# A two-layer mixer with an expert-lookup feed-forward: gate products ordered behind the low parts, wider one-hots, modulation steps spread

## The chip, the core and the metric

The kernel is one program on one core of a Trainium2 chip. The core has five engines that run side by side, each taking its own instructions in order: TensorE (PE, matmuls; PEld is its weight load), VectorE (DVE), ScalarE (ACT), GpSimd (POOL) and SyncE (SP), which here issues most transfers between DRAM and on-chip memory. The metric is the device time of one execution in microseconds (us), taken as the median of runs. A profiler's trace of one execution is beside it.

## The reference

Two layers work on 256 tokens `x` of width 1024 and, in the first layer, on 256 context tokens as well. Each layer is a mixer of four branches, then a feed-forward that looks up experts; both are scaled and shifted by six modulation vectors per stream.

```python
for l in range(DEPTH):                      # 2
    mx = (jax.nn.silu(c) @ mod_w[l] + mod_b[l])[:, None, :]      # six vectors of 1024
    mc = (jax.nn.silu(c_ctx) @ mod_w[l] + mod_b[l])[None, None, :]
    ...
    yx, yc = hybrid_mixer(hx, hc, ...)
    x = x + g1x * yx
    hx2 = rmsnorm(x, norm2_w[l]) * (1.0 + sc2x) + sh2x
    x = x + g2x * peer_ffn(hx2, peer_w_q[l], peer_keys[l], peer_u[l], peer_v[l])

def one_block(xt):                          # of peer_ffn, 128 tokens
    q = (xt @ w_q).reshape(128, 8, 2, 64)
    s = jnp.einsum('thpd,hpkd->thpk', q, keys)
    s1, i1 = lax.top_k(s[:, :, 0], 16)
    s2, i2 = lax.top_k(s[:, :, 1], 16)
    ...                                     # the 16 best of 16 x 16 sums, per head
    g = jax.nn.softmax(top_s, axis=-1)
    act = gelu(einsum('td,thkd->thk', xt, u[eidx]))
    return einsum('thk,thkd->td', g * act, v[eidx])
```

There are 128 x 128 experts, and each token has 8 heads of 16 chosen ones.

## The kernel before

**Dense experts.** The kernel doesn't gather the rows of `u` and `v` for most token tiles. It computes all 16384 experts in 128 blocks of 128 and multiplies by a gate matrix that is zero for experts not chosen. The first pass (`block` in `peer_u`, the U pass) computes `gelu(u x)` for block e and writes it to DRAM (`act_d`). The second pass (`peer_v`, the V pass) loads it back as tile `a`, multiplies it by the gates `G` (line 1241, the gate product), splits the product into `wh` and `wl`, and multiplies by block e of `v` into `pacc`, which stays in PSUM. In layer 0 three token tiles go this way (`n` = 384) and one goes through gathered rows (`sparse`, lines 900 to 931): 256 gathers of 512 KB, a multiply on VectorE for each, spread over the blocks of both passes. In layer 1 there are two tiles (`n` = 256).

**Two halves of each weight.** A weight block of 128 x 1024 floats is loaded into `raw` (three buffers) by `next_w`, and `split_w` (lines 150 to 158) makes `hi` on ScalarE and the low part `lo = raw - hi` on VectorE (line 157), five buffers each. Each product takes three matmuls: both high, and the two mixed ones. A V block is 18 matmuls of 512 columns in layer 0 and 12 in layer 1. The handle `lo_turn["last"]` keeps the last low part that was traced.

**Blocks and pairs.** In layer 0 a tile `a` holds two blocks (a pair), in layer 1 four (a quad, two gate products). There are four buffers for `a` in layer 0 and two in layer 1, where every fourth quad stays on chip instead (`keep`). The load of a later `a` (line 1213, on SP's queue) is traced behind the `wl` (line 1246) that is the last reader of its buffer. `G` comes in four parts for every 16 blocks.

**Who orders the work.** The text of the kernel gives the order of tracing. The framework's scheduler then sets the order on each engine by its own estimate of when an instruction is ready, so one that is ready early may be put in front. `with tc.issue_after(ins):` adds an edge of order to what is traced inside it: on the engine of `ins`, it is issued behind `ins`, with no wait for its end. The kernel uses it already for the multiplies of the gathered rows (lines 919 and 929).

**Gates.** For each token tile `route` finds the chosen experts; then `hot` (16 times a tile, in the U pass) builds, for 8 tokens, the one-hot of the second index (`a2`) and that of the first index (`a1`), and from the latter its products with the high and the low part of the weight (`bh`, `bl`). `eight` multiplies them on TensorE into the gates of those tokens, which go to `g_d`. The indices and weights lie along the free axis in `ix`, which `look2` fills from PSUM.

**Modulation.** Four of layer 0's segments and two of layer 1's are computed in layer 0's mixer without TensorE's weight path: `mod_seg` (lines 242 to 277) loads a half segment in eight pieces of 256 KB and folds each into `macc` on VectorE for both streams; `finish` sums over partitions by four transposes for each stream on TensorE. The generator stops twice in a segment. `with_mods` takes one step of it at the given indices of a filler generator (`MODS_AT`, and line 709); what is left is taken behind the last merge (line 846), ahead of the output projection `out_proj`. Of the 13 steps that exhaust the six segments, layer 0's mixer takes 2 + 3 + 4 + 2 = 11 at indices and the others behind the last merge.

Of the kernel before, what the change touches and what calls it, by code (L numbers as in the profile page):

```python
# [19 lines left out]
P = 128  # L20
# [10 lines left out]
SP = 1  # L31
NG = 4
AB = (4, 2)
MODS_AT = (((1, 5, 8), (1, 6, 12, 17), (0, 2)), ((1, 8), (1, 12), (2,)))
GS = 16384.0
MLA_SCALE = 96.0 ** -0.5

# [76 lines left out]
def hybrid_peer(ctx, tc, resin, cvec, modw, modb, nw, win, uq, uk, uv, colw, nab, retl, gnw,  # L114
# [159 lines left out]
    def with_mods(gen, at, mod):  # L274
        for i, x in enumerate(gen):
            if i in at:
                next(mod, None)
            yield
# [98 lines left out]
    def mixer(l, hT, st, s_acc, pre):  # L377
# [328 lines left out]
                yield  # L706
            yield from proj_tok(B_NV, range(4), lambda t2, p: act.activation(nv[:, t2:t2 + 2, :], p, AF.Copy))

        weave(retention(), with_mods(fill_na(), (0, 3, 6) if not full else (0, 5), mods), 0.7)
        rs.close()  # L710

        acp = s_acc.enter_context(tc.tile_pool(name=f"acp{l}", bufs=1, reuse_waits="tile", side="right"))
# [220 lines left out]
    def peer_u(l, hT, rp, ap_, pre, kp_, normed, xrow, vps):  # L933
# [30 lines left out]
        def route(tt):  # L964
# [95 lines left out]
            def look2():  # L1060
                if tt not in dense:
                    wn = T[tt, "wn"]
                    spw["idx"] = kp_.tile([P, P], U32, name="idx")
                    spw["wgt"] = kp_.tile([P, P], F32, name="wgt")
                    dve.scalar_tensor_tensor(wn[:, 0], wn[:, 0], float(P), wn[:, 1], op0=OP.mult, op1=OP.add)
                    dve.tensor_copy(spw["idx"], wn[:, 0])
                    dve.tensor_copy(spw["wgt"], wn[:, 2])
                    return
                tp = ps_o("idxT")
                for q in range(3):  # L1070
                    pe.transpose(tp[:, q * P:(q + 1) * P], T[tt, "wn"][:, q], ident)
                ix = up2.tile([P, 4, P], F16, tag="ixT", bufs=2, name="ixT")
                act.activation(ix[:, 0:2].rearrange("p q t -> p (q t)"), tp[:, :256], AF.Copy)
                act.activation(ix[:, 2], tp[:, 256:384], AF.Copy, scale=GS)
                dve.scalar_tensor_tensor(ix[:, 3], tp[:, 256:384], GS, ix[:, 2], op0=OP.mult, op1=OP.subtract)
                T[tt, "ix"] = ix
            add(400, look2)
            if tt not in dense:
# [1 line left out]
            for c in range(8):  # L1080
                def gsub(c=c):
                    T[tt, "stage"] = up2.tile([P, P, 16], F32, tag="gst", bufs=2, name="gst")
                add(0, gsub)
                for j in range(2):
                    def hot(c=c, j=j):
                        t0 = c * 16 + j * 8
                        ix = T[tt, "ix"]
                        cur = [ix[:, q, t0:t0 + 8].rearrange("p (g t) -> p g t", t=2)[:, :, None, :]
                               .to_broadcast([P, 4, P, 2]) for q in range(4)]
                        irep = irep2[:, None].to_broadcast([P, 4, P, 2])  # L1090
                        a2, a1, bh, bl = (up2.tile([P, 4, P, 2], F16, tag=nm, bufs=nb, name=nm)
                                          for nm, nb in (("a2", 2), ("a1", 1), ("bh", 2), ("bl", 2)))
                        dve.tensor_tensor(a2, irep, cur[1], op=OP.is_equal)
                        dve.tensor_tensor(a1, irep, cur[0], op=OP.is_equal)
                        dve.tensor_tensor(bh, a1, cur[2], op=OP.mult)
                        dve.tensor_tensor(bl, a1, cur[3], op=OP.mult)
                        T[tt, "hot", c, j] = a2, bh, bl, T[tt, "stage"]

                    def eight(c=c, j=j):
                        a2, bh, bl, stage = T.pop((tt, "hot", c, j))  # L1100
                        for q in range(2):
                            gp = ps_s("gps")
                            for i in range(4):
                                t = q * 4 + i
                                o = gp[:, i * P:(i + 1) * P]
                                at = a2[:, t // 2, :, t % 2]
                                pe.matmul(o, at, bh[:, t // 2, :, t % 2], start=True, stop=False)
                                pe.matmul(o, at, bl[:, t // 2, :, t % 2], start=False, stop=True)
                            tc0 = j * 8 + q * 4
                            act.activation(stage[:, :, tc0:tc0 + 4],  # L1110
                                           gp.rearrange("p (t i) -> p i t", t=4), AF.Copy)
                        if j == 1:
                            sync.dma_start(g_d[tt * 8 + c], stage)

                    add(2800, hot)
                    if "late" in T:
                        add(0, T.pop("late"))
                    T["late"] = eight
# [70 lines left out]
    def peer_v(l, vp, tail, s_up, keep, sparse_step, gen):  # L1189
# [42 lines left out]
        for e in range(P):  # L1232
# [3 lines left out]
            if e % na == 0:  # L1236
                ia = e // na
                a, G = keep[ia] if ia in keep else loads.pop(ia), loads["G", i]
                for j in range(0, na, 2):
                    a4 = a[:, j:j + 2].rearrange("p j (c t) -> p j c t", t=16)  # L1240
                    dve.tensor_tensor(a4, a4, G[:, :, e % ng + j:e % ng + j + 2].rearrange("p c j t -> p j c t"),  # L1241
                                      op=OP.mult)
                wh = vp.tile([P, na, n], F32R, tag="wh", bufs=3, name="wh")
                wl = vp.tile([P, na, n], F32R, tag="wl", bufs=3, name="wl")
                act.activation(wh, a, AF.Copy)
# [256 lines left out]
```

## Time and profile before

| | |
|---|---|
| median of 3 runs | 3072.34 us (3067.71 to 3074.73) |
| profiled execution, its own time | 3068.09 us |
| its span, first to last instruction | 3066.3 us |
| TensorE matmuls open | 2912.8 us, 95% of the span |
| TensorE weight loads | 84% |
| VectorE busy | 2287.7 us, 75% |
| ScalarE busy | 1293.5 us, 42% |
| GpSimd busy | 442.8 us, 14% |
| transfers | 718.42 MB, mean 234 GB/s |
| chain that ended last | PE 34%, transfers 16% (`a<-act_d` alone 10%), DVE 15% |

How to read it: matmuls are pipelined and overlap, so a busy TensorE need not be one at its best. The chain is followed back from the last instruction, at each step to what released it. The share of a transfer in it is time in which nothing else stood between the kernel and its end.

### The profile page before, as it was taken

Reading aid. Unit: us, or ns where it says so; the run is one execution under the profiler, and the core shown is the slowest. Engines: PE = TensorE matmul, PEld = TensorE weight load, DVE = VectorE, ACT = ScalarE, POOL = GpSimd, SP = SyncE. Lnnn points to the kernel's source line nnn. Section 1 sums busy time; section 2 is a strip of 40 time slices with the busy share of each in tenths; the row PEclk is TensorE's granted clock in tenths of the full one; section 3 lists DMA queues with packets and bytes.
Section 4 is the critical chain, followed back from the end, with each engine's and each line's share of the span. In section 5 each row is a group of like instructions: output and inputs, shape, how many; then the busy total and the mean of one; then the engine's idle time right before and its main releaser. Section 6 shows DMA issues by size and latency. Waiting matters only on the chain.

```text
span 3066.3 us, 46551 instructions
## 1 busy us (share of the span) xinstructions
PE 2912.8 (95%) x17771; PEld 2563.2 (84%) x17771; DVE 2287.7 (75%) x4013; ACT 1293.5 (42%) x1910; POOL 442.8 (14%) x378
## 2 busy tenths in 40 slices
PE   8999999799999999998888999999999999999998
PEld 6877767798889989986677777988899999988887
DVE  6768793658989999666666777777659798576665
ACT  6344442433343434332232233545554545554443
POOL 0200011001222232232222322101100000000000
PEclk9999999899999999999999999999999999999999
DMA  6343333435797979998888887465455867898874
GB/s 250 108 145 124 117 124 103 149 116 201 238 331 245 351 258 351 359 380 300 295 303 300 316 275 264 163 211 174 138 167 188 272 213 269 288 312 290 272 257 152
DMA packets 242080, 718.42 MB, mean 234 GB/s; under 512 B 24384, under 2 KB 68544, under 8 KB 236736
## 3 DMA queue, kind: packets, MB, share of 16 engines
q1 hardware_dynamic: 204704, 580.69, 56.1%
q0 software_dynamic: 36864, 134.23, 12.3%
q8 instruction: 139, 2.28, 0.3%
q14 instruction: 85, 0.70, 0.1%
q10 hardware_dynamic: 288, 0.52, 0.0%
HBM read 633.56 MB, written 81.79 MB: 233 GB/s over the span
## 4 chain that ended last, share of the span: by engine, by line
PE 34%; DMA 16%; DVE 15%; issue 4%; ACT 2%; POOL 0%; DVEq 0%; SPq 0%; POOLq 0%; ACTq 0%
PE va L1229 12%; DMA a<-act_d 10%; DVE lo L157 4%; PE H L358 4%; PE H L360 4%; PE H L359 4%; DMA raw<-in_ub_dram 4%; DVE spacc L930 2%; DVE wl L1246 2%; DMA mraw<-in_modw_dram 1%; PE proj L358 1%; PE proj L359 1%; PE proj L360 1%; DVE gat L920 1%; ACT hi L154 1%
## 5 line engine op out<-in xcount | busy, mean ns | idle before, releaser
L154 ACT ACTIVATE hi<-raw 128x1024 fp32r<-128x1024 f32 x676 | 715.7, 1060 | 1345.6 <-DMA raw<-in_vb_dram 451.6
L157 DVE TENSOR_TENSOR lo<-raw,hi 128x1024 fp32r<-128x1024 f32 x680 | 832.2, 1226 | 375.2 <-ACT hi L154 370.9
L358 PE MATMUL H<-h2h,hi 128*128 128x384 f32 (+1 forms) x2048 | 647.9, 316 | 14.7 <-ACT ast L1146 14.7
L360 PE MATMUL H<-h2h,lo 128*128 128x384 f32 (+1 forms) x2048 | 637.1, 312 | 2.5 <-DVE lo L157 2.4
L359 PE MATMUL H<-h2l,hi 128*128 128x384 f32 (+1 forms) x2048 | 637.7, 311 | 0.0
L1229 PE MATMUL va<-lo,wh 128*128 128x512 f32 x1280 | 408.3, 398 | 55.5 <-DVE lo L157 55.1
L358 PEld LDWEIGHTS H<-h2h,hi 128*128 128x128 f32 x2048 | 388.3, 190 | 20.2 <-ACT ast L1146 18.2
L1229 PE MATMUL va<-hi,wh 128*128 128x512 f32 x1280 | 403.4, 394 | 1.6 <-ACT keep L1146 1.5
L1229 PE MATMUL va<-hi,wl 128*128 128x512 f32 x1280 | 402.8, 394 | 0.0
L360 PEld LDWEIGHTS H<-h2h,lo 128*128 128x128 f32 x2048 | 387.6, 189 | 4.1 <-DVE lo L157 3.6
L359 PEld LDWEIGHTS H<-h2l,hi 128*128 128x128 f32 x2048 | 388.6, 190 | 0.0
L1229 PEld LDWEIGHTS va<-lo,wh 128*128 128x128 f32 x1280 | 241.8, 191 | 119.0 <-DVE lo L157 70.3
L1229 PEld LDWEIGHTS va<-hi,wh 128*128 128x128 f32 x1280 | 243.1, 190 | 53.9 <-ACT keep L1146 2.4
L358 PE MATMUL proj<-hh,hi 128*128 128x256 f32 (+1 forms) x808 | 283.1, 351 | 5.3 <-ACT hh L349 3.4
L1229 PEld LDWEIGHTS va<-hi,wl 128*128 128x128 f32 x1280 | 244.0, 191 | 52.0
L359 PE MATMUL proj<-hl,hi 128*128 128x256 f32 (+1 forms) x808 | 276.4, 342 | 0.0
L360 PE MATMUL proj<-hh,lo 128*128 128x256 f32 (+1 forms) x808 | 275.8, 342 | 0.0
L1241 DVE TENSOR_TENSOR a<-a,G 128x768 f32<-128x768 f32 (+1 forms) x112 | 92.2, 842 | 208.6 <-DMA a<-act_d 200.1
L910 POOL DMA_INDIRECT gat<-in_urow_dram,idx x128 | 161.1, 1259 | 536.2 <-DVE gat L920 348.6
L910 POOL DMA_INDIRECT gat<-in_vb_dram,idx x128 | 161.7, 1263 | 412.6 <-DVE spacc L930 396.4
L252 DVE SCALAR_TENSOR_TENSOR macc<-mraw,cs,macc 128x512 f32<-128x512 f32 x224 | 167.4, 781 | 41.2 <-DMA mraw<-in_modw_dram 39.7
L358 PEld LDWEIGHTS proj<-hh,hi 128*128 128x128 f32 x808 | 152.9, 190 | 27.7 <-issue 4.0
(301 smaller groups left out, 4370.4 us busy)
## 6 DMA issues: line engine op xcount, KB each, us to landing
raw<-in_ub_dram SPq DMA_DIRECT2D x256, 512.0 KB, 5.0
raw<-in_vb_dram SPq DMA_DIRECT2D x256, 512.0 KB, 4.9
raw<-in_win_dram SPq DMA_DIRECT2D x112, 512.0 KB, 4.0
mraw<-in_modw_dram SPq DMA_DIRECT2D x160, 256.0 KB, 2.9
g_d<-gst SPq DMA_DIRECT2D x40, 1024.0 KB, 5.5
act_d<-ast SPq DMA_DIRECT2D x64, 384.0 KB, 5.0
a<-act_d SPq DMA_DIRECT2D x64, 384.0 KB, 5.5
G<-g_d SPq DMA_DIRECT2D x32, 768.0 KB, 10.8
```

The source lines that it names most:

```text
L154: act.activation(hi, raw, AF.Copy)
L157: lo_turn["last"] = dve.tensor_tensor(lo, raw, hi.bitcast(F32), op=OP.subtract)
L252: dve.scalar_tensor_tensor(acc[st], w, cs[:, k, st:st + 1], acc[st], op0=OP.mult, op1=OP.add)
L358: pe.matmul(o, a, hh[:, k, c0:c1], start=(k == 0), stop=False)
L359: pe.matmul(o, a, hl[:, k, c0:c1], start=False, stop=False)
L360: pe.matmul(o, b, hh[:, k, c0:c1], start=False, stop=(k == KD - 1))
L910: pool.indirect_dma_start(buf[j], None, urow if j < P else vrow, bass.IndirectOffsetOnAxis(ap=idx[:, k:k + 1], axis=0))
L920: dve.scalar_tensor_tensor(g, g, 1.0, xrow, op0=OP.mult, op1=OP.mult, accum_out=hk[:, 0, k:k + 1])
L930: dve.scalar_tensor_tensor(acc[0], g, hk[:, 1, k:k + 1], acc[0], op0=OP.mult, op1=OP.add)
L1229: pe.matmul(pacc[tt][h], x[:, tsl], y[:, h * 512:(h + 1) * 512], start=(e == 0 and x is wh and y is vh), stop=(e == P - 1 and x is wl))
L1241: dve.tensor_tensor(a4, a4, G[:, :, e % ng + j:e % ng + j + 2].rearrange("p c j t -> p j c t"), op=OP.mult)
L1246: dve.tensor_tensor(wl, a, wh.bitcast(F32), op=OP.subtract)
```

## The change

The gate products are traced inside `tc.issue_after` of the last low part, which at that place is the one of the block before the pair or quad. In `hot`, both one-hots are made by one comparison over eight planes (four of the first index, four of the second), in a tile of two buffers; the two products with the weight's parts go to the halves of one tile. For that `ix` has the four kinds side by side for every eight tokens, and `look2` fills it with three evacuations instead of two. In layer 0 the indices at which modulation steps are taken become (0, 4, 8), (1, 4, 7, 11), (1, 6, 11, 16) and (0, 3): 13 steps.

```diff
--- before.py
+++ after.py
@@ -31,7 +31,7 @@
 SP = 1
 NG = 4
 AB = (4, 2)
-MODS_AT = (((1, 5, 8), (1, 6, 12, 17), (0, 2)), ((1, 8), (1, 12), (2,)))
+MODS_AT = (((1, 4, 7, 11), (1, 6, 11, 16), (0, 3)), ((1, 8), (1, 12), (2,)))
 GS = 16384.0
 MLA_SCALE = 96.0 ** -0.5
 
@@ -706,7 +706,7 @@
                 yield
             yield from proj_tok(B_NV, range(4), lambda t2, p: act.activation(nv[:, t2:t2 + 2, :], p, AF.Copy))
 
-        weave(retention(), with_mods(fill_na(), (0, 3, 6) if not full else (0, 5), mods), 0.7)
+        weave(retention(), with_mods(fill_na(), (0, 3, 6) if not full else (0, 4, 8), mods), 0.7)
         rs.close()
 
         acp = s_acc.enter_context(tc.tile_pool(name=f"acp{l}", bufs=1, reuse_waits="tile", side="right"))
@@ -1069,10 +1069,12 @@
                 tp = ps_o("idxT")
                 for q in range(3):
                     pe.transpose(tp[:, q * P:(q + 1) * P], T[tt, "wn"][:, q], ident)
-                ix = up2.tile([P, 4, P], F16, tag="ixT", bufs=2, name="ixT")
-                act.activation(ix[:, 0:2].rearrange("p q t -> p (q t)"), tp[:, :256], AF.Copy)
-                act.activation(ix[:, 2], tp[:, 256:384], AF.Copy, scale=GS)
-                dve.scalar_tensor_tensor(ix[:, 3], tp[:, 256:384], GS, ix[:, 2], op0=OP.mult, op1=OP.subtract)
+                ix = up2.tile([P, 16, 4, 8], F16, tag="ixT", bufs=2, name="ixT")
+                tq = tp[:, :384].rearrange("p (q c t) -> p q c t", q=3, t=8)
+                act.activation(ix[:, :, 0], tq[:, 0], AF.Copy)
+                act.activation(ix[:, :, 1], tq[:, 1], AF.Copy)
+                act.activation(ix[:, :, 2], tq[:, 2], AF.Copy, scale=GS)
+                dve.scalar_tensor_tensor(ix[:, :, 3], tq[:, 2], GS, ix[:, :, 2], op0=OP.mult, op1=OP.subtract)
                 T[tt, "ix"] = ix
             add(400, look2)
             if tt not in dense:
@@ -1083,18 +1085,16 @@
                 add(0, gsub)
                 for j in range(2):
                     def hot(c=c, j=j):
-                        t0 = c * 16 + j * 8
                         ix = T[tt, "ix"]
-                        cur = [ix[:, q, t0:t0 + 8].rearrange("p (g t) -> p g t", t=2)[:, :, None, :]
-                               .to_broadcast([P, 4, P, 2]) for q in range(4)]
-                        irep = irep2[:, None].to_broadcast([P, 4, P, 2])
-                        a2, a1, bh, bl = (up2.tile([P, 4, P, 2], F16, tag=nm, bufs=nb, name=nm)
-                                          for nm, nb in (("a2", 2), ("a1", 1), ("bh", 2), ("bl", 2)))
-                        dve.tensor_tensor(a2, irep, cur[1], op=OP.is_equal)
-                        dve.tensor_tensor(a1, irep, cur[0], op=OP.is_equal)
-                        dve.tensor_tensor(bh, a1, cur[2], op=OP.mult)
-                        dve.tensor_tensor(bl, a1, cur[3], op=OP.mult)
-                        T[tt, "hot", c, j] = a2, bh, bl, T[tt, "stage"]
+                        cur = [ix[:, c * 2 + j, q:q + 2].rearrange("p q (g t) -> p (q g) t", t=2)[:, :, None, :]
+                               .to_broadcast([P, 8, P, 2]) for q in (0, 2)]
+                        irep = irep2[:, None].to_broadcast([P, 8, P, 2])
+                        a = up2.tile([P, 8, P, 2], F16, tag="a12", bufs=2, name="a12")
+                        bb = up2.tile([P, 8, P, 2], F16, tag="bhl", bufs=2, name="bhl")
+                        dve.tensor_tensor(a, irep, cur[0], op=OP.is_equal)
+                        for q in range(2):
+                            dve.tensor_tensor(bb[:, q * 4:q * 4 + 4], a[:, :4], cur[1][:, q * 4:q * 4 + 4], op=OP.mult)
+                        T[tt, "hot", c, j] = a[:, 4:], bb[:, :4], bb[:, 4:], T[tt, "stage"]
 
                     def eight(c=c, j=j):
                         a2, bh, bl, stage = T.pop((tt, "hot", c, j))
@@ -1238,8 +1238,9 @@
                 a, G = keep[ia] if ia in keep else loads.pop(ia), loads["G", i]
                 for j in range(0, na, 2):
                     a4 = a[:, j:j + 2].rearrange("p j (c t) -> p j c t", t=16)
-                    dve.tensor_tensor(a4, a4, G[:, :, e % ng + j:e % ng + j + 2].rearrange("p c j t -> p j c t"),
-                                      op=OP.mult)
+                    with tc.issue_after(inst(lo_turn["last"])):
+                        dve.tensor_tensor(a4, a4, G[:, :, e % ng + j:e % ng + j + 2]
+                                          .rearrange("p c j t -> p j c t"), op=OP.mult)
                 wh = vp.tile([P, na, n], F32R, tag="wh", bufs=3, name="wh")
                 wl = vp.tile([P, na, n], F32R, tag="wl", bufs=3, name="wl")
                 act.activation(wh, a, AF.Copy)
```

## Rows read from the trace of the kernel before

**Rows 1.** Windows: engines' busy us and instructions, granted clock, transfer share, GB/s.

```profile
core 0: us, PE busy (x) PEld busy (x) DVE busy (x) ACT busy (x) POOL busy (x), PEclk, DMA share, GB/s
1347.00:1894.00 547.00, 491.45 (x2056) 393.96 (x2055) 379.22 (x350) 163.32 (x172) 154.41 (x121) 0.96 0.86 301
2800.00:2900.00 100.00, 100.00 (x443) 82.81 (x442) 66.39 (x66) 47.83 (x46) 0.00 (x0) 1.00 0.83 276
1200.00:1280.00 80.00, 77.76 (x526) 76.39 (x525) 56.88 (x82) 33.09 (x52) 24.08 (x19) 1.00 1.01 381
...
560.00:570.00 10.00, 9.25 (x63) 8.96 (x64) 7.30 (x13) 2.77 (x4) 0.00 (x0) 0.80 0.25 98
...
200.00:500.00 300.00, 298.86 (x1480) 214.76 (x1475) 226.35 (x418) 134.93 (x247) 30.26 (x26) 1.00 0.38 122
```

**Rows 2.** Waits from 1347 to 1894 us: total us, times, longest us.

```profile
DVE a L1241 <- DMA a<-act_d: 175.2, 55, 8.6
...
PE va L1229 <- DVE lo L157: 55.1, 30, 6.5
```

**Rows 3.** The chain of waits, 1540 to 1570 us: start, us, what.

```profile
1545.26 0.88 DVE wl L1246
...
1546.16 7.21 DMA a<-act_d
```

**Rows 4.** VectorE's timeline, same place: start, us, instruction, idle before it.

```profile
1553.46 0.96 DVE L1241 TENSOR_TENSOR a<-a,G 128x768 f32<-128x768 f32 x1 [5.00 <-DMA a<-act_d]
1554.34 1.22 DVE L157 TENSOR_TENSOR lo<-raw,hi 128x1024 fp32r<-128x1024 f32 x1
```

**Rows 5.** Windows of line 157 (low parts) alone, from the start.

```profile
0.00:1700.00 1700.00, 380.83 (x311) 0.97 0.68 235
0.00:2900.00 2900.00, 784.74 (x642) 0.98 0.69 236
```

**Rows 6.** Windows of line 1241 (gate products) alone, from the start.

```profile
0.00:1700.00 1700.00, 41.38 (x44) 0.97 0.68 235
```

**Rows 7.** Windows of line 1229 (second pass's matmuls) alone, by layer.

```profile
1200.00:1700.00 500.00, 338.68 (x1418) 272.07 (x1419) 0.97 0.91 326
2200.00:2900.00 700.00, 191.53 (x843) 158.14 (x844) 1.00 0.75 249
```

**Rows 8.** Transfers issued from 1347 to 1894 us: KB each, median us to landing.

```profile
raw<-in_vb_dram SPq DMA_DIRECT2D x113, 512.0 KB, 5.4
...
G<-g_d SPq DMA_DIRECT2D x24, 768.0 KB, 9.1
```

**Rows 9.** Windows of 20 us in layer 0's second pass, columns as rows 1.

```profile
1360.00:1380.00 20.00, 20.00 (x90) 16.57 (x89) 12.98 (x12) 5.72 (x6) 4.96 (x4) 1.00 1.02 374
...
1740.00:1760.00 20.00, 13.92 (x53) 10.73 (x52) 10.36 (x11) 3.91 (x4) 4.92 (x4) 0.83 0.96 342
```

**Rows 10.** Lines by shape, layer 1's second pass: busy us, mean ns, idle.

```profile
L1246 DVE TENSOR_TENSOR wl<-a,wh 128x1024 fp32r<-128x1024 f32 x22 | 26.9, 1223 | 12.0 <-ACT wh L1245 12.0
L1245 ACT ACTIVATE wh<-a 128x1024 fp32r<-128x1024 f32 x21 | 22.3, 1060 | 14.8 <-PE va L1229 14.7
```

**Rows 11.** TensorE's waits in layer 0's mixer and after, 90 to 760 us.

```profile
PE modt L261 <- DVE macc L252: 16.9, 2, 16.3
```

**Rows 12.** TensorE's timeline where the output projection begins.

```profile
561.41 0.56 PE L877 MATMUL wo<-hi,ah 128*128 128x256 f32 x1
```

**Rows 13.** ScalarE's timeline at the same place.

```profile
543.10 4.25 ACT L857 ACTIVATE ah<-acc 128x512 fp32r<-128x512 f32 x8
```

**Rows 14.** VectorE's timeline in one group of one-hots.

```profile
2642.40 0.68 DVE L1093 TENSOR_TENSOR a<-irep,ixT 128x1024 f16<-128x1024 f16 x1
2643.00 0.68 DVE L1095 TENSOR_TENSOR bh<-a,ixT 128x1024 f16<-128x1024 f16 x1
```

**Rows 15.** VectorE's timeline around a 2048-element comparison.

```profile
2365.78 1.21 DVE L1049 TENSOR_TENSOR oh<-abf,ib 128x2048 bf16<-128x2048 bf16 x1
2366.92 0.28 DVE L1056 TENSOR_TENSOR wn<-oh 128x128 f32<-128x128 bf16 x1
```

## The prediction, before the result was known

> **What bounds the kernel now.** I read the page first: TensorE has matmuls open for 95% of the span, VectorE for 75%, and the chain names `a<-act_d`, a DRAM transfer, for 10% of the span. An average cannot say where that 10% lies, so next came the stage view [rows 1]. The reader is to compare two stretches of the same code, layer 0's second expert pass (1347 to 1894 us) and layer 1's (2800 to 2900). Layer 1 issues 443 matmuls in 100 us, 0.2257 us each, at clock 1.00. Layer 0 issues 2056 matmuls of the same shape in 547 us, 0.2660 us each, at clock 0.96. At 18 matmuls a block that is 114 blocks, or 57 pairs, at 9.58 us a pair; at layer 1's pace a pair needs 8.13. 2056 x 0.2257 = 464.1 us, so the stretch holds 547 - 464.1 = 82.9 us that TensorE would not need.
>
> The waits of that stretch tell what takes it [rows 2]: VectorE's gate product (L1241) waits 175.2 us in 55 waits for its `a` tile, while TensorE waits for low parts (L157). The chain shows the loop [rows 3]: `wl` of one pair ends at 1546.14, the load of an `a` starts at 1546.16, lands 7.21 us later, and the product starts. VectorE takes its instructions in order, so the low part behind the product, which TensorE needs, starts only after it [rows 4]. Why is the product in front at all? The counts [rows 5, 6] show it. At 1700.0 us VectorE has done 311 - 16 - 216 = 79 low parts of this pass (16 belong to the two opening modulation segments, 216 to the blocks of layer 0 before this pass). It has done 44 products, the last for blocks 86 and 87. So the product runs seven blocks ahead of the low parts, right behind the `wl` that frees its buffer (four `a` buffers), and each pair pays a whole landing in the open. TensorE stands at block 1418 / 18 = 78.8 [rows 7]: no low part is in hand. In layer 1 at 2900.0 there are 642 - 16 - 552 = 74 low parts and TensorE is at 843 / 12 = 70.2: 3.8 blocks in hand, no stall.
>
> **The change, part by part. The tie.** Each product gets an order edge behind the low part of the block before its own. It adds no instruction. The product of pair n then runs behind low part 2n - 1, seven low parts later, about 3.5 pairs or 30 us. Its load is still issued behind `wl` of pair n - 4, about four pairs (33 us) before it is wanted; the longest product wait is 8.6 us [rows 2]. So the wait goes, and low parts run as far ahead as five `hi`/`lo` buffers and three raw buffers let them. What is late next? Either TensorE, or the transfers. At best, all 82.9 us go. The worst I can argue is that the stalls around the `G` loads stay: 24 such loads [rows 8] come as six groups of four, one to 16 blocks. In the window 1740 to 1760 [rows 9], the deepest of them, 53 matmuls ran where 20 / 0.2257 = 88.6 fit, so 35.6 x 0.2257 = 8.0 us were lost. Six times 8.0 is 48, which leaves 35 us of gain. Between 35 and 83 I go by the row nearest to a full TensorE beside full transfers: 1200 to 1280 [rows 1], where the transfer share is 1.01 at 381 GB/s and matmuls are open for 77.76 / 80 = 97.2%. 464.1 / 0.972 = 477.5, a gain of **69.5 us**. The stretch moves 301 GB/s x 547 us = 165 MB, so it would need 345 GB/s; window 1360 to 1380 moved 374 in this very stage with 90 matmuls in 20 us [rows 9].
>
> TensorE's busy row gives a smaller bound for the same stretch, 547 - 491.45 = 55.6 us idle [rows 1]. The Trainium skill (Perfetto Trace Analysis, Identifying the Most-Contended Engine) says that matmul busy time misjudges the distance to the roofline and that weight-load busy time is to be used. By it 393.96 / 0.828 = 475.8 us would be needed, a gain of 71, and the term would be 71 instead of the 55.6 that the busy row would allow. The matmul counts side with the rule, because a matmul at clock 0.96 counts as busy.
>
> In layer 1 the same tie takes away a reserve instead of a stall. A quad's chain behind low part 4m - 1 is two products (at most the 0.88 of a layer 0 product each [rows 4]), `wh` 1.06 and `wl` 1.22 [rows 10], with one other ACT pass (1.06) and one low part (1.22) between: 6.3 us. In hand are 3.8 + 1 blocks of 12 x 0.2257 = 2.71 us, 13 us. I cost it at nothing; with the cover gone (no low part in hand) it would be 6.3 - 2.7 = 3.6 us for each of 32 quads.
>
> **The modulation segments.** Twelve half segments are loaded and folded by VectorE. Today eleven steps are taken inside the mixer and the twelfth load comes behind the last merge. There TensorE waits 16.3 us for `macc` [rows 11] in front of the output projection, whose first matmul comes at 561.41 [rows 12]. After the change thirteen steps lie inside, so nothing remains. The projection's left operand (`ah`, eight passes from 543.10) can then let TensorE start at about 543.7, one pass (4.25 / 8 us) after their begin [rows 13]: 17.7 us. To this come 10 x (1 - 0.80) = 2.0 us of half clock in 560 to 570 [rows 1], less 8 x 0.23 = 1.8 us for the last eight transposes (an estimate, a matmul slot each), which TensorE must now do between merges, and about 1 for what a moved half costs there (below): **17 us**. The moved loads (16 x 256 KB on SP's queue, in front of `win` blocks) and their folds go to stretches like 200 to 500 [rows 1], where transfers fill 0.38, VectorE three quarters, and TensorE lost 300 - 298.86 = 1.1 us beside the halves that pass there now. That is the cover; were each of the two moved halves to cost the whole 1.1, 15 us would be left. Upper end 19, if the transposes cost nothing.
>
> **The one-hots.** Two 1024-element compares become one of 2048. The pitch of a compare is 0.60 [rows 14], of a 2048-element one 1.14 [rows 15]: 2 x 0.60 - 1.14 = 0.06 us, for 48 hots in layer 0 and 32 in layer 1 (there TensorE is full, so nothing). 48 x 0.06 = 2.9 us of VectorE if all of it sets the pace, nothing if none does; I take **2**. The third small evacuation on ACT (five times in all, under 0.5 us each) lies beside matmuls, on an engine that the page shows busy for 42% of the span. The Trainium skill (VectorE: DVE Perf Modes, the TRN2 errata section) puts the fixed part of an instruction at about 150 cycles, 0.156 us, by which the term would be 7.5; the pitch in the rows is smaller, since the next instruction starts before the last one's record ends.
>
> Sum: 69.5 + 17 + 2 = 88.5. The profiled execution took 3068.1 us (span 3066.3), 4.2 below the median of the three runs, 3072.3, so 2979.6 for its like and **2984 us** for the median.
>
> **The rivals.** (A) *Transfers take the place of the wait.* For: the share is 0.86 already and 0.96 in the deepest of the bad windows; raw loads have only three buffers. Against: the full windows of rows 9. Then the tie gives 35, with 17 and no gain from the hots: 3072 - 52 = 3020. (B) *The tie does nothing:* low parts are late by their own raw loads, and the product only stands where VectorE would idle anyway. For: the page's chain has raw loads and low parts next to the `a` loads, and a raw load takes 5.4 us to land [rows 8]. Against: raw loads wait for VectorE's low part to free a buffer, and layer 1 loads them faster. 3072 - 19 = 3053. (C) *SP's queue turns the tie into a longer loop, and the kernel gets slower.* The `a` load waits on SP for `wl`, now behind the tie, and holds what stands behind it. If raw 2n + 1 stood behind the load that waits for `wl` of pair n, a pair would cost product 0.88, `wh` 1.06, `wl` 0.88 [rows 3, 4, 10], landing 5.4 [rows 8], `hi` 1.06 and `lo` 1.22 = 10.5 us instead of 9.58: 57 x 0.92 = 52 more, 3072 + 52 - 19 = 3105. A pair of the forecast takes 477.5 / 57 = 8.38, so each pair so caught costs 2.1, and the kernel is slower once 88.5 / 2.1 = 42 of the 57 are. Against: raw 2n + 1 is free to go at low part 2n - 2, before that `wl` can run. (D) *No change:* a smaller loop of that kind, or a new order of the first expert pass, eats the gain.
>
> **How the numbers follow.** The forecast 0.67 (its own range 2964 to 3000: 83 or 57 for the tie, the rest at its ends), A 0.19, B 0.06, C 0.06, D 0.02. The range runs from 2960 to 3030: it holds the forecast and A, and leaves out B, C and D, 0.14, and a little at the low end. Faster by over 0.2% (6 us, about what a measurement of this kernel can tell from no change): 0.67 + 0.19 + 0.06 = 0.92; within 0.2%: 0.02; slower: 0.06.
>
> **What would show it.** Tie right: product waits for `a` near zero, 79 low parts beside some 40 products, a low part two or more blocks before its matmuls, the layer 0 pass under 490 us for 2056 matmuls. Rival A: TensorE waits for low parts behind ACT's waits for raw loads, in bursts. Segments right: no TensorE gap near 542, none over 3 us earlier. One-hots right: 80 compares of 2048 near 1.21 us. Wrong as a whole: SP's queue stuck on `wl` in most pairs, or layer 1's pass below 440 matmuls in 100 us.

## The result, and the profile after

The changed kernel takes 2972.9 us, median of four runs (2967.1 to 2976.1), beside 3070.0 for the kernel before in the same comparison: a ratio of 0.968, interval 0.966 to 0.970. The profiled execution spans 2971.7 us against 3066.3. The predicted time was 2984.

First the stage view of the changed kernel, columns as in [rows 1]. The first line is layer 0's second pass between its 6th and its 120th block, the second is layer 1's, the third the mixer, the fourth the start of the output projection.

```profile
core 0: us, PE busy (x) PEld busy (x) DVE busy (x) ACT busy (x) POOL busy (x), PEclk, DMA share, GB/s
1336.10:1801.20 465.10, 465.10 (x2054) 385.12 (x2053) 387.29 (x357) 167.19 (x174) 208.74 (x121) 1.00 0.98 358
2700.00:2800.00 100.00, 100.00 (x443) 82.81 (x442) 67.09 (x66) 47.51 (x47) 0.00 (x0) 1.00 0.83 277
200.00:500.00 300.00, 297.70 (x1476) 213.08 (x1475) 228.96 (x423) 137.13 (x249) 31.89 (x25) 1.00 0.39 120
546.00:556.00 10.00, 8.55 (x70) 8.15 (x69) 8.64 (x12) 7.19 (x13) 2.18 (x1) 1.00 0.74 269
```

The same matmuls that took 547 us at clock 0.96 [rows 1] take 465.1 us at clock 1.00: 465.1 / 2054 = 0.2264 us each, within 0.3% of layer 1's 0.2257. Of the 82.9 us that TensorE did not need, about 1 is left (465.1 beside 464.1). Transfers fill 0.98 of that stretch and stop nothing; these are windows of 100 us within it:

```profile
1400.00:1500.00 100.00, 100.00 (x443) 82.81 (x442) 86.30 (x80) 36.35 (x38) 48.49 (x29) 1.00 1.01 376
1500.00:1600.00 100.00, 100.00 (x443) 82.81 (x442) 80.88 (x75) 35.97 (x38) 44.75 (x27) 1.00 0.99 365
1600.00:1700.00 100.00, 100.00 (x442) 82.78 (x442) 83.38 (x77) 35.11 (x37) 43.43 (x27) 1.00 1.01 373
```

The page's chain by engine and by line. `a<-act_d`, 10% of the span before, is gone from it, and `va` matmuls stand in its place.

```profile
PE 71%; DVE 14%; DMA 8%; issue 4%; ACT 3%; POOL 1%; SPq 0%; ACTq 0%; POOLq 0%; DVEq 0%
PE va L1229 29%; PE H L358 5%; PE H L360 5%; PE H L359 5%; DMA raw<-in_ub_dram 5%; DVE lo L157 4%; PE proj L358 4%; PE proj L359 3%; PE proj L360 3%; DMA mraw<-in_modw_dram 2%; DVE macc L252 1%; PE sc L464 1%; ACT hi L154 1%; DVE gat L920 1%; PE attno L497 1%
```

VectorE's timeline at the place of [rows 4] (the product is now line 1242, `wl` 1247), and SP's queue beside it:

```profile
1539.93 0.94 DVE L1242 TENSOR_TENSOR a<-a,G 128x768 f32<-128x768 f32 x1
1540.80 1.21 DVE L157 TENSOR_TENSOR lo<-raw,hi 128x1024 fp32r<-128x1024 f32 x1
1541.93 0.94 DVE L1247 TENSOR_TENSOR wl<-a,wh 128x768 fp32r<-128x768 f32 x1
...
1547.06 0.95 DVE L1242 TENSOR_TENSOR a<-a,G 128x768 f32<-128x768 f32 x1
1548.80 1.22 DVE L157 TENSOR_TENSOR lo<-raw,hi 128x1024 fp32r<-128x1024 f32 x1 [0.79 <-ACT hi L154]
```

```profile
1542.03 0.33 SPq L162 DMA_DIRECT2D raw<-in_vb_dram  x1
1542.90 0.33 SPq L1213 DMA_DIRECT2D a<-act_d  x1
```

No product waits. In the whole stretch VectorE's only wait of over 5 us in sum is this one, where the 175.2 us for `a` [rows 2] stood before (engine, line, what for: total us, times, longest):

```profile
DVE lo L157 <- ACT hi L154: 81.4, 52, 8.3
```

The load of an `a` still goes out as `wl` ends (1541.93 + 0.94 = 1542.87), but its product comes some pairs later. The raw load goes out at 1542.03, as the low part that frees its buffer ends, and is not held behind the load of `a`.

The counts to 1700.0 us of low parts and of products (DVE busy, its instructions, clock, transfers), and of the second pass's matmuls from 1200.0 on (PE and PEld busy):

```profile
0.00:1700.00 1700.00, 404.42 (x331) 0.99 0.71 251
0.00:1700.00 1700.00, 47.46 (x50) 0.99 0.71 251
1200.00:1700.00 500.00, 389.48 (x1717) 322.36 (x1718) 1.00 1.00 373
```

That is 331 - 16 - 216 = 99 low parts beside 50 products: two blocks a product, no more. Before it was 79 beside 44 [rows 5, 6]. TensorE stands at block 1717 / 18 = 95.4, so 3.6 blocks of low parts are in hand where there were none.

TensorE's timeline at the output projection, where the gap of [rows 11] was. The first `wo` matmul comes at 546.94 instead of 561.41, right behind the last transposes; a wait of 1.29 us follows.

```profile
545.24 1.95 PE L288 MATMUL gp<-consts,modc 128*128 128x128 f32 x16
546.94 0.36 PE L877 MATMUL wo<-hi,ah 128*128 128x256 f32 x1
...
549.61 0.39 PE L879 MATMUL wo<-hi,al 128*128 128x256 f32 x1 [1.29 <-DVE al L858]
```

By the first matmul of each stage in the two traces, the difference of the spans, 94.6 us, falls like this (the first 0.3 lies ahead of the mixer):

| stretch | before, us | after, us | difference |
|---|---|---|---|
| mixer, from 37.9 (37.5 after) to the first `wo` | 523.5 | 509.4 | -14.1 |
| from there to layer 0's first expert pass | 104.9 | 105.5 | +0.6 |
| first pass, 112 blocks | 583.3 | 590.3 | +7.0 |
| its last 16 blocks, to the second pass | 72.9 | 67.7 | -5.2 |
| second pass, first six blocks | 24.8 | 24.8 | 0.0 |
| second pass, 114 blocks | 546.4 | 465.1 | -81.3 |
| the rest, with layer 1 | 1172.7 | 1171.3 | -1.4 |

### The profile page after: what moved, and what is told of

Same layout as the page of the kernel before. It is cut to its first block, busy times and chain, and to the rows that moved or that the text cites. A ratio compares the mean times of both kernels' runs of the same rounds, so it can differ in the third digit from the quotient of the medians.

```text
span 2971.7 us, 46328 instructions
## 1 busy us (share of the span) xinstructions
PE 2890.0 (97%) x17771; PEld 2556.9 (86%) x17771; DVE 2286.6 (77%) x3933; ACT 1297.4 (44%) x1917; POOL 516.2 (17%) x378
## 4 chain that ended last, share of the span: by engine, by line
PE 71%; DVE 14%; DMA 8%; issue 4%; ACT 3%; POOL 1%; SPq 0%; ACTq 0%; POOLq 0%; DVEq 0%
PE va L1229 29%; PE H L358 5%; PE H L360 5%; PE H L359 5%; DMA raw<-in_ub_dram 5%; DVE lo L157 4%; PE proj L358 4%; PE proj L359 3%; PE proj L360 3%; DMA mraw<-in_modw_dram 2%; DVE macc L252 1%; PE sc L464 1%; ACT hi L154 1%; DVE gat L920 1%; PE attno L497 1%
## 5 line engine op out<-in xcount | busy, mean ns | idle before, releaser
L358 PE MATMUL H<-h2h,hi 128*128 128x384 f32 (+1 forms) x2048 | 647.9, 316 | 14.1 <-ACT ast L1146 14.1
L1229 PE MATMUL va<-lo,wh 128*128 128x512 f32 x1280 | 397.5, 389 | 0.0
L910 POOL DMA_INDIRECT gat<-in_urow_dram,idx x128 | 174.6, 1364 | 522.8 <-DVE gat L920 335.4
L910 POOL DMA_INDIRECT gat<-in_vb_dram,idx x128 | 217.6, 1700 | 263.7 <-DVE spacc L930 241.0
L300 POOL TENSOR_TENSOR rs<-rs,mhalf 128x1 f32<-128x1 f32 x16 | 10.1, 634 | 963.1 <-DVE rs L297 929.0
```

Of the source, the lines that this page charges most:

```text
L300: pool.tensor_tensor(r[:, 1:2], r[:, 0:1], mhalf, op=OP.pow)
L358: pe.matmul(o, a, hh[:, k, c0:c1], start=(k == 0), stop=False)
L910: pool.indirect_dma_start(buf[j], None, urow if j < P else vrow, bass.IndirectOffsetOnAxis(ap=idx[:, k:k + 1], axis=0))
L1229: pe.matmul(pacc[tt][h], x[:, tsl], y[:, h * 512:(h + 1) * 512], start=(e == 0 and x is wh and y is vh), stop=(e == P - 1 and x is wl))
```

## The experiments

The kernel before took 3056.5 us beside runs 1 to 4, 3054.5 beside 5 to 8 and 3064.7 beside 9 to 11, each group on a chip of its own, so each ratio is to the kernel before on the same chip.

### 1 to 4: the parts alone

**Tie alone:** only the edge around the product.

```diff
+                    with tc.issue_after(inst(lo_turn["last"])):
...
```

> Only the tie of the gate products; one-hots and modulation steps as before. Theory (the open landing of each a tile in VectorE's order is the whole stall of layer 0's second pass): that pass falls from 546 to 465 us for 114 blocks, and about 5 us go at the border of the passes, where the first product no longer waits for G in front of low parts of the first pass; ratio about 0.972 (3070 to 2984). Rival (transfers become the bound and the tie alone would leave the bursts): ratio 0.985 or more.

Measured: 2986.2 us, ratio 0.977 (0.975 to 0.979), a gain of 70 us where some 85 were expected. Its second pass is not what falls short. In the window of the same 114 blocks it takes the time of the whole change to the digit; the untied pass that it is measured against is shorter here, as the next run shows.

```profile
1347.20:1812.30 465.10, 465.10 (x2053) 385.12 (x2052) 386.49 (x356) 166.42 (x173) 207.28 (x121) 1.00 0.97 359
```

**Modulation steps alone:**

```diff
-MODS_AT = (((1, 5, 8), (1, 6, 12, 17), (0, 2)), ((1, 8), (1, 12), (2,)))
+MODS_AT = (((1, 4, 7, 11), (1, 6, 11, 16), (0, 3)), ((1, 8), (1, 12), (2,)))
...
-        weave(retention(), with_mods(fill_na(), (0, 3, 6) if not full else (0, 5), mods), 0.7)
+        weave(retention(), with_mods(fill_na(), (0, 3, 6) if not full else (0, 4, 8), mods), 0.7)
```

> Only the modulation steps spread. Theory: the 16.3 us gap in front of the output projection goes, some 2 to 3 us come back as small stalls earlier; 14 us less, ratio 0.9955. Rival (the steps cost elsewhere what they save at the end): ratio 0.999 or more.

Measured: 3048.3 us, ratio 0.998 (0.996 to 0.999), a gain of 4 to 11 us, between the 14 of the theory and the 3 of its rival. The first `wo` matmul comes at 548.8 us here and at 547.7 in the run with tie and steps, against 558.6 and 560.1 in the two runs without the new steps: 10 to 12 us earlier. The untied second pass, in its window and its wait:

```profile
1341.60:1868.60 527.00, 487.24 (x2054) 392.05 (x2053) 379.06 (x350) 163.77 (x172) 154.50 (x121) 0.97 0.89 312
```

```profile
DVE a L1241 <- DMA a<-act_d: 154.5, 55, 8.1
```

The untied pass takes 527.0 us here, not 546, with the same 55 waits, 20.7 us shorter in sum; the one-hots run, on the same chip, has 527.3. The tied pass takes 465.1 in every trace without added loads, so the tie is worth 62 us here and 81 in the first comparison. The chip is the likely reason for the difference, but with one trace of the kernel before it is not shown.

**One-hots alone:** one compare of 2048 and the layout of `ix` that it needs.

```diff
-                        dve.tensor_tensor(a2, irep, cur[1], op=OP.is_equal)
-                        dve.tensor_tensor(a1, irep, cur[0], op=OP.is_equal)
...
+                        dve.tensor_tensor(a, irep, cur[0], op=OP.is_equal)
...
```

> Only the one-hots in one comparison. The trace after has the first pass of layer 0 up to block 112 at 590 us where it was 583. Theory of the prediction: 2 us less, ratio 0.999. Rival (the wider one-hots cost the first pass time, since one instruction now waits for the buffers that both halves of the old pair shared out): 4 to 7 us more, ratio 1.0015 to 1.0025.

Measured: 3057.7 us, ratio 1.001 (0.999 to 1.003): no gain of over 2 us. The interval reaches from 2 us less to 8 more, so it decides neither for the theory nor for its rival.

**Without the one-hots:** tie and modulation steps.

```diff
+                    with tc.issue_after(inst(lo_turn["last"])):
...
+MODS_AT = (((1, 4, 7, 11), (1, 6, 11, 16), (0, 3)), ((1, 8), (1, 12), (2,)))
...
```

> The change without its one-hots. If the one-hots cost 4 to 7 us, this is at ratio 0.966, ahead of the whole change's 0.968; if they gain 2, it is at 0.969.

Measured: 2971.4 us, ratio 0.972 (0.971 to 0.974). On top of the tie the modulation steps bring 2986.15 - 2971.43 = 14.7 us.

### 5 to 8: the whole change again, buffers and transfers

**The whole change, unaltered:**

> The whole change once more, on the chip of the next three and beside the kernel before, since two chips gave the kernel before 3070 and 3056 us. Theory: with the tie no landing is in the open, so this kernel takes 2970 to 2975 us on any chip, whatever the kernel before takes there.

Measured: 2967.3 us, 3 under the range expected, ratio 0.972 (0.970 to 0.973), the same as without the one-hots within the intervals.

**Two buffers for `a` instead of four, without and with the tie.** If the wait comes from running ahead as far as the buffers reach, fewer buffers alter where it falls, but not that a product stands right behind the `wl` that frees its buffer.

```diff
-AB = (4, 2)
+AB = (2, 2)
```

Kernel before with it:

> The kernel before with two buffers for a in layer 0 instead of four. Theory (the product stands right behind the wl that frees its buffer, whatever their number, and pays one landing a pair): the same as the kernel before, ratio 0.995 to 1.01. Rival (the wait is a matter of how many loads are in flight): with half of them the wait about doubles, ratio 1.03 or more.

Changed kernel with it:

> The whole change with two buffers for a in layer 0. A load is then issued two pairs, 16 us, before its product, and a landings in the pass have a median of 7 us. Theory (order, not number of buffers): as the whole change, ratio to the kernel before 0.966 to 0.974, the product's wait under 10 us in all. Rival: the tie works only with four loads in flight, 0.98 or more.

Measured: 3072.3 us untied, ratio 1.007 (1.004 to 1.009), and 2966.8 tied, ratio 0.971 (0.969 to 0.973). The 114 blocks take 524.7 us untied and 465.1 tied. VectorE's largest wait in the untied second pass, and its timeline there:

```profile
DVE a L1241 <- DMA a<-act_d: 147.2, 54, 6.0
```

```profile
1553.49 0.96 DVE L1241 TENSOR_TENSOR a<-a,G 128x768 f32<-128x768 f32 x1 [5.36 <-DMA a<-act_d]
1554.36 1.22 DVE L157 TENSOR_TENSOR lo<-raw,hi 128x1024 fp32r<-128x1024 f32 x1
```

So it is the place in the order that exposes each landing, not how many buffers there are; with the tie, two buffers are enough.

**More transfers:** the changed kernel with two `a` buffers, and, traced with each block of layer 0's second pass, a load of 256 KB into scratch that feeds nothing.

```diff
+            if full:
+                xt = vp.tile([P, 512], F32, tag="xt", bufs=4, name="xt")
+                sync.dma_start(xt, vb[l, e][:, :512])
```

> The run with two a buffers and the tie, and in layer 0's second pass one more load of 256 KB for each block, into a scratch tile that nothing reads (32 MB in all). Each block then needs 1.75 MB in 4.06 us, 431 GB/s, where the best window moved 402. If transfers are at their limit in the pass now (share 0.99 to 1.01), the pass grows by the bytes over 375 to 400 GB/s: 114 blocks take 499 to 532 us instead of 465, some 40 to 75 us for the whole pass. If the share overstates the load, under 15 us.

Measured: 3030.4 us, ratio 0.992 (0.990 to 0.994). The 114 blocks take 510.5 us; below them are ScalarE's wait for raw loads in the pass (150.2 us in the whole change), TensorE's longest two, and SP's own for its scratch tiles.

```profile
1349.40:1859.90 510.50, 487.24 (x2053) 386.00 (x2052) 386.70 (x356) 166.58 (x173) 201.90 (x121) 0.98 1.01 382
```

```profile
ACT hi L154 <- DMA raw<-in_vb_dram: 276.0, 88, 10.2
PE va L1229 <- ACT hi L154: 9.9, 7, 2.7
PE va L1229 <- DVE lo L157: 5.8, 12, 0.5
```

```profile
SPq L1254 <- DMA xt<-in_vb_dram: 106.2, 58, 5.9
```

This is what rival A would look like, if less in low parts than in high ones. But the scratch ring itself held SP's queue for 106 us, so part of the loss may be the ring's; run 11 asks again with half the bytes and twice the tiles, and shows when the added loads of both runs went out.

### 9 to 11: price of the one-hots, slack of the tie, room of the transfers

**Split one-hots:** the changed kernel with four compares and four products of 512 elements a group.

```diff
-                        dve.tensor_tensor(a, irep, cur[0], op=OP.is_equal)
-                        for q in range(2):
-                            dve.tensor_tensor(bb[:, q * 4:q * 4 + 4], a[:, :4], cur[1][:, q * 4:q * 4 + 4], op=OP.mult)
+                        for q in range(0, 8, 2):
+                            dve.tensor_tensor(a[:, q:q + 2], irep[:, :2], cur[0][:, q:q + 2], op=OP.is_equal)
+                        for q in range(0, 8, 2):
+                            dve.tensor_tensor(bb[:, q:q + 2], a[:, q % 4:q % 4 + 2], cur[1][:, q:q + 2], op=OP.mult)
```

> The whole change, but each group of one-hots is made by four compares and four products of 512 elements instead of one compare of 2048 and two products of 1024. If an instruction costs VectorE a fixed 0.06 us beside its elements (2 x 0.60 - 1.14 = 0.06 by the pitches before), the five added ones cost 0.3 us a group, some 15 us of VectorE over the 48 groups of layer 0's first expert pass and 10 us over the 32 of layer 1. Theory 1: VectorE sets the pace of layer 0's first pass, and the one-hots' saving was real but too small to be seen; then this kernel is 10 to 15 us slower than the whole change (2977 to 2983 where that takes 2967). Theory 2: VectorE has slack around the groups, which wait for the matmuls that free their buffers, so their length changes nothing by itself; then it is within 4 us of the whole change.

Measured: 2989.3 us, ratio 0.975 (0.973 to 0.977), 13.5 us above run 10, in which the one-hots are as changed (0.9715, 0.9695 to 0.9734; the two intervals just touch). The whole change itself was not timed on this chip, and run 10 has a looser tie as well, which costs its second pass nothing (465.1 us). First the 112 blocks of the first pass in this run, then those of run 10:

```profile
653.00:1250.20 597.20, 554.05 (x3587) 535.56 (x3586) 562.38 (x1576) 223.11 (x340) 148.48 (x111) 0.98 0.78 270
```

```profile
653.40:1244.00 590.60, 554.82 (x3589) 537.42 (x3587) 548.47 (x1340) 224.58 (x343) 157.61 (x113) 0.97 0.79 278
```

VectorE is 13.9 us busier, in 236 more instructions, 0.059 us each; the pass and its last 16 blocks together take 11.8 us longer (670.3 against 658.5; 665.5 is the most in any other kernel with the tie). VectorE is busy for 93% of the 112 blocks in run 10. This speaks for a price near the one-hots' own length and against the second theory, but the same work took the tied kernels 651.6 to 665.5 us there, so the place of the loss rests on one trace and is not shown.

**Tie four blocks looser:** the product goes behind low part 2n - 5 instead of 2n - 1.

```diff
-                    with tc.issue_after(inst(lo_turn["last"])):
+                    with tc.issue_after(inst(lo_turn["all"][-5])):
```

> The whole change, but the edge goes to the low part that was traced four blocks earlier: the product for blocks 2n and 2n + 1 is put behind low part 2n - 5 instead of 2n - 1, so still ahead of four low parts that it could have stood behind. Theory 1: what counts is that the load's landing (5 to 9 us) lies between the issue of the product and the wl that freed its buffer; four blocks are two pairs, 16 us, ahead of need, and the load was issued about four pairs ahead, so about two pairs remain for it: no product waits for its load, and the time is that of the whole change within 5 us. Theory 2: only the full distance hides a landing beside full transfers (median 7 us, some 13): then products wait again in part of the pairs, and 10 to 40 us of the gain go.

Measured: 2975.7 us, ratio 0.972 (0.970 to 0.973). The second pass takes 465.1 us, and no product waits for its `a` in it. Most of the distance is reserve.

**Some more transfers:** as run 8, with 128 KB a block in a ring of eight.

```diff
+                xt = vp.tile([P, 256], F32, tag="xt", bufs=8, name="xt")
+                sync.dma_start(xt, vb[l, e][:, :256])
```

> The whole change with two buffers for a instead of four in layer 0, and in each block of layer 0's second pass one load more, of 128 KB into a ring of eight scratch tiles, which feeds nothing. The pass moves some 1.44 MB a block in all (345 to 375 GB/s); with it, at 18 x 0.2257 = 4.06 us a block, about 32 GB/s more, or 380 to 405. Theory 1: the transfers of the whole change still have room up to the 388 to 396 GB/s that were moved with the load of 256 KB: the pass stays within 5 us of 465 us for 114 blocks. Theory 2: they are at their bound at the share of 1.0 that the whole change shows: 128 KB over 374 GB/s is 0.35 us a block, 40 us over 114 blocks. Between them lies a bound of 390: by the amount that is asked above it, 0 to 18 us.

Measured: 3001.1 us, ratio 0.979 (0.977 to 0.981), 25 us above run 10. First the 114 blocks, then two windows of them:

```profile
1353.10:1839.10 486.00, 474.17 (x2053) 383.84 (x2053) 386.30 (x356) 166.50 (x173) 215.09 (x121) 1.00 1.00 369
```

```profile
1400.00:1500.00 100.00, 91.94 (x379) 70.19 (x378) 71.69 (x67) 29.73 (x32) 30.70 (x22) 0.98 1.04 385
...
1600.00:1700.00 100.00, 100.00 (x443) 82.81 (x442) 80.43 (x76) 35.13 (x37) 52.25 (x26) 1.00 1.01 375
```

The loads did not go out one a block, in this run or in run 8. SP issued all 128 of them early (run 11, then run 8; ns from shortest to longest, first and last start in us):

```profile
L1254 SPq DMA_DIRECT2D xt<-in_vb_dram x128: 327/346/1707, 1272.3 to 1520.4; - x128
L1254 SPq DMA_DIRECT2D xt<-in_vb_dram x128: 327/328/1490, 1267.3 to 1660.8; - x128
```

Cut there, the passes look like this (run 11 in two parts, then run 8 in two, and a window of run 8):

```profile
1353.10:1520.00 166.90, 157.71 (x667) 124.30 (x666) 117.22 (x107) 50.47 (x53) 57.54 (x38) 0.99 1.03 378
1520.00:1839.10 319.10, 316.47 (x1386) 259.54 (x1387) 269.08 (x249) 116.03 (x121) 157.55 (x83) 1.00 0.99 364
1349.40:1660.00 310.60, 289.22 (x1190) 224.70 (x1189) 217.28 (x199) 93.26 (x97) 99.50 (x69) 0.97 1.03 392
1660.00:1859.90 199.90, 198.01 (x865) 161.30 (x864) 169.42 (x158) 73.32 (x76) 102.40 (x52) 1.00 0.98 366
1400.00:1500.00 100.00, 92.60 (x379) 71.63 (x378) 69.31 (x64) 29.96 (x31) 30.19 (x23) 0.97 1.04 396
```

At 0.2264 us each, 667 matmuls need 151.0 us, so 15.9 of the 21 us were lost while the added loads went out; in run 8, 1190 need 269.4, and 41.2 of 45 were lost. So the mean of a whole pass, 369 or 382 GB/s, is no bound. While loads were added, windows moved 385 and 396 GB/s with 379 matmuls where 443 fit; without them run 11's windows of 375 and 378 GB/s lost nothing. The added loads also stood in SP's queue, 106.2 us for their ring in run 8 and 10.3 in run 11, so what the transfers' room costs and what the queue costs is not separated.

## Why the prediction was right, and where a term was off

**The tie: mechanism right, price 12 us too low.** The product stood in front of the low part that TensorE needed, and the edge put it behind; the parts alone, the buffer pair and the looser tie all say so. The forecast took 477.5 us for the pass, from 1200 to 1280 [rows 1], read as the price of a full TensorE beside full transfers. The pass took 465.1, so the tie brought 81.3 instead of 69.5 there. The row was the wrong one. In that window of the kernel before, TensorE's only wait is this:

```profile
PE gps L1107 <- ACT gst L1110: 2.2, 1, 2.2
```

It is a wait of the first pass's gates for an evacuation on ScalarE, and it makes the whole 80 - 77.76 us. No transfer is in it, and the second pass has no such instruction. The row to ask was one of the same stage: the window 1360 to 1380 [rows 9], 90 matmuls in 20 us at share 1.02, cited only as support, shows the final pace. By the weight-load time of the Trainium skill (Perfetto Trace Analysis, Identifying the Most-Contended Engine) the tie would have brought 71 us, nearly as far off: the 2053 weight loads took 385.1 us after the change, not the 394.0 of before, since they too were longer at clock 0.96. The same section of the Trainium skill names the arithmetic done, over what the peak could do, beside weight-load time. A count of matmuls at layer 1's pace is a measure of that kind: it gave 464.1, and the trace agrees with that.

**A gain that the prediction did not have.** Before, the first product of the second pass stood on VectorE while it waited 6.4 us for its `G` tiles, with a low part of the first pass and the multiply of a gathered row behind it:

```profile
1288.16 0.96 DVE L1241 TENSOR_TENSOR a<-a,G 128x768 f32<-128x768 f32 x1 [6.44 <-DMA G<-g_d]
1289.04 1.22 DVE L157 TENSOR_TENSOR lo<-raw,hi 128x1024 fp32r<-128x1024 f32 x1
```

This is the border row of the table, -5.2 us. It fits the runs: 67.6 to 70.1 us in those with the tie and unsplit one-hots, 72.9 to 76.6 in those without the tie.

**Modulation segments: right, 14 instead of 17.** The gap is gone: TensorE's idle time in the mixer fell from 25.8 to 11.2 us. The projection begins at 546.94 instead of the 543.7 forecast: TensorE's other stalls there grew from 25.8 - 16.3 = 9.5 to 11.2, by 1.7 us, where 1 was allowed, and the last transposes and the branch matmuls end later. The half clock of [rows 1] (560 to 570) did go, as the last line of the stage view shows (1.00), but the wait for `al` keeps that window at 8.55 us busy, and the stretch to the first pass is no shorter. Alone the steps brought 4 to 11 us (run 2), on top of the tie 14.7 (run 4); the intervals are too wide to call these different.

**One-hots: 2 forecast, none measured.** The price per group was right. The line groups of the changed kernel:

```profile
L1094 DVE TENSOR_TENSOR a<-irep,ixT 128x2048 f16<-128x2048 f16 x80 | 97.4, 1219 | 19.9 <-PE gps L1108 13.2 <-ACT ixT L1075 6.5
L1096 DVE TENSOR_TENSOR bhl<-a,ixT 128x1024 f16<-128x1024 f16 x160 | 102.8, 684 | 1.0
```

In the 112 blocks one-hots take 119.8 us of VectorE after and 122.8 before, 3.0 less against 2.9 worked out. The idle time in front of the compares, mostly for the `gps` matmuls that free their tiles, lies between 9 and 20 us in either form. If run 9 is taken at its word, time of VectorE in this pass has a price near 1; but with the one-hots unsplit its 112 blocks take anything from 583 to 595 us in the twelve traces, so 3 us can't be seen there. The Trainium skill (VectorE: DVE Perf Modes, the TRN2 errata section) gives the fixed part twice: 58 cycles in its table, and about 150 as measured in the duration of a single instruction. At 0.96 GHz, its clock for VectorE, that is 0.060 and 0.156 us, and by these estimates the 236 instructions that run 9 added would take 14 or 37 us. The trace has 13.9, so in a stream the smaller one holds, and the prediction's 7.5 us went by the other.

**Layer 1: zero, and it is zero.** 443 matmuls in 100 us, as before.

**The rivals.** A did not come true, but its bound is near: the pass asks for 358 GB/s, its windows run full at up to 376, and with loads added windows of 385 and 396 ran 379 matmuls where 443 fit. That the transfers' room takes the difference, and not the added loads' place in SP's queue, is argued and not shown. B and D fell with the first run. C did not occur: raw loads leave when their buffer is free, and SP's queue stands less on the load of `a` than it did, as its own waits before and after show.

```profile
SPq L1213 <- DVE wl L1246: 134.3, 56, 8.9
SPq L1213 <- DVE wl L1247: 34.3, 52, 4.1
```

So before, the load of `a` also held the queue in front of raw loads, which the prediction did not count for that kernel. It was not what came last: there VectorE's low parts waited only 0.5 us for their high parts, against 175.2 for the product in front. The transfer share gives little warning: TensorE is full at 1.01 and far from it at 1.04.

The sum of forecast terms, 88.5, stands beside 94.6 in the two profiled spans and 97 between the medians. The tie was 17 us too low (12 in the pass, 5 at its border), the segments and one-hots 5 too high, and 7 us went the other way in the first pass, within its spread of 583 to 595; about 1 lies in the rest.

## What to carry to other kernels

When an engine that takes its instructions in order waits for a load at nearly every turn, look at where the waiting instruction stands: right behind the one that frees its buffer means that each landing is paid, with four buffers (175.2 us in 55 waits) as with two (147.2 in 54), and an edge that sends it back a few turns makes the load early. Price the cure by the matmul count at the pace of an undisturbed stretch of the same code, and before a row is used as the price of a bound, ask what that row waits for. A saving below the spread of its stage (here 3 us in 583 to 595) will be shown by no run, even on an engine that is 93% busy. When loads are added to probe a bound, look first at when they were issued: two runs here meant one a block and got all of them in the first part of the pass.

## What the runs showed of the hardware

The transfer share passes 1.0 without any loss: TensorE ran full over 100-us windows at 365 to 376 GB/s while the median landing of an `a` in the pass grew from 5.2 to 6.4 us, and the queue of loads issued ahead covered it. The Trainium skill (Perfetto Trace Analysis, Roofline) says that a core alone may pull more than its share of 358 GB/s, with some 435 as the ceiling of its engines. The trace agrees on the first; the second was not reached here, where 396 is the most that a window of 100 us moved, at a share of 1.04 and with TensorE short of work (run 8).

An exposed wait differs from trace to trace where a hidden one does not: the same untied pass took 546 us in the first trace, with 175.2 us of waits for `a`, and 527 in two traces of another comparison, with 154.5 and 155.2, while the tied one took 465.1 on three chips and in the first comparison. Whether the chip makes the difference is not shown. Merging two f16 compares of 1024 elements into one saves VectorE 0.06 us (3.0 us over 48 groups), and splitting them costs the same for each added instruction (13.9 us over 236).
